# Branch gates by one Strassen level with token sums kept in DRAM, the Fourier transform beside them and its projection behind them; retention in step and a joined qkv projection

## The chip, the cores and the metric

The kernel runs on one core of a Trainium2 chip. The metric is device time in microseconds (us) of one execution, the median of the runs shown. All data are float32. A product of two float32 matrices is made of three TensorE matmuls over a high and a low part (hi·hi, hi·lo, lo·hi), each part in the chip's fp32r form; `split` makes the parts, the high one by a copy on ScalarE (ACT), the low one by a subtraction on VectorE (DVE).

## The reference

One layer of a hybrid backbone on 1024 tokens of width 1024 (and 256 context tokens). Cut to what matters here:

```python
h = modulate(rms_norm(x, norm1_w), sh1, sc1)
q, k, v, g, f = split_proj(h @ w_in)            # 8 heads of 64 (q, k) and 128 (v); f is 512 wide
o = bidir_retention(rope(q), rope(k), v, ...)   # chunks of 128, starts from the context's states
ret_d  = (layer_norm_per_head(o) * silu(g)) @ w_ret_out
four_d = real(fft2(f, tokens and groups of 128)) @ w_four_out
gates  = sigmoid(h @ w_branch_gate + b)         # (1024, 2048): g_r, g_f
x = x + g1 * ((g_r * ret_d + g_f * four_d) @ w_out)
x = x + g2 * conv_ffn(modulate(rms_norm(x, norm2_w), sh2, sc2))
return rms_norm(x, final_norm_w)
```

sh1, sc1, g1, sh2, sc2, g2 are six vectors of 1024 that come from `silu(c) @ w_mod + b_mod`.

## The kernel before, in words

Everything is kept transposed (channels on the 128 partitions, tokens along the free axis), in two halves t of 512 tokens. The normalized input is `hT[t]`, a hi and a lo tile of 8 channel blocks by 512 tokens each, in the pool `ap` (four buffers with the tag A, all taken by hT).

The program's stages, in the order in which they are written:

1. Norm, modulation and the first head pair's q, k and v (to about 85 us of the trace).
2. `gate_proj(0)`, the context's keys and values (`ctx_proj`, `ctx_state`, four pairs), the decay tables (`decay_tables`, `expo`).
3. For the head pairs p = 1 to 3: q and k (`in_proj` with `w_qk`), then v (`in_proj` with `w_v`), each as matmuls of 128 tokens by 256 columns; `gate_proj(p)`; `retention(p)`. The scheduler lays retention of pair p beside the projections of pair p + 1.
4. The retention gates `gr` (L588, L592): 8 blocks of 128 channels, each 2 halves x 8 channel blocks x 3 parts = 48 matmuls of 512 tokens; the sigmoid goes to `sr_d` in DRAM.
5. The Fourier branch: projection `f`, `spectra`, `transform`, `nyquist`; its result z stays in SBUF. Then, in turns, a Fourier gate `gf` (48 matmuls of 512) and a block `fo` of the projection of z (24 matmuls), multiplied on DVE and written to `t_d` in DRAM.
6. "re", the retention projection, merged with `sr_d` and `t_d`; then "wo", the output projection with the residual, and the second norm, for each half.
7. The FFN: the up projection by one level of Strassen's scheme in Winograd's form (`up_mm`, `chain` at L775: seven chains of 12 matmuls of 512 for a pair of blocks), the convolution, the gate; then the down projection by the same scheme (L1054).

The vectors g1, sc2, sh2 and g2 are made on DVE: `mod_dot` makes one of their 32 blocks from 512 KB of `w_mod` (a DMA into the raw buffer `wraw`, two multiply-and-sum passes of 512, one small step). `run_mods(n)` takes the next n of them; the table MODS says how many are taken where. When the block of g1 or g2 is complete, TensorE transposes the 8 columns (`gt`) and the row goes to DRAM.

The order on each engine is made by a scheduler at build time from the written program; each engine then runs its own list in order, and so do the two queues that issue DMAs (SP, and POOL where the code says `G.dma_start`). Weights come through three raw buffers `wraw` of 512 KB (`wload`, L102) into two buffers `whi` and two `wlo`.

Of the kernel before, what the change touches and what calls it, by code (L numbers as in the profile page):

```python
# [16 lines left out]
P = 128  # L17
# [14 lines left out]
MODS = (2, 2, 2, 2)  # L32
# [11 lines left out]
def tile_block(ctx: ExitStack, tc: tile.TileContext, a: dict, out: bass.AP):  # L44
# [49 lines left out]
    sr_d = dr.tile([KD, P, L], F32, name="sr_d")  # L94
    t_d = dr.tile([KD, P, L], F32, name="t_d")
# [259 lines left out]
    T2 = {"t2": 3, "t2b": 3}  # L355
    with tc.tile_pool(name="rp", bufs=1) as rp:
# [29 lines left out]

        def in_proj(wk, t, ps):
            for n in range(4):
                for k in range(KD):
                    mm3(ps[:, n, :], pick(hT[t], ALL, k, blk(n)), wk(k), k == 0, k == KD - 1)  # L390
# [39 lines left out]
        def retention(p, qkr, vt, tab, sg):  # L430
# [37 lines left out]
            for t in range(2):  # L468
                scs = [rt(f"sc{p}{i}{t}") for i in range(2)]
                for n in range(4):  # L470
                    c = blk(4 * t + n)
                    for i in range(2):
                        T.matmul(scs[i][:, blk(n)], kT[blk(i, QK), c], qT[blk(i, QK), c], start=True, stop=True)
                for i in range(2):
                    h, sc = 2 * p + i, scs[i]
                    pt = t2(rp, f"pt{h}{t}").rearrange("p (n c) -> p n c", n=4)
                    tt(pt, sc.rearrange("p (n c) -> p n c", n=4),
                       tab[:, i, :].unsqueeze(1).broadcast_to([P, 4, P]), MUL)
                    o = rt(f"o{h}{t}")
                    for n in range(4):  # L480
                        T.matmul(o[:, blk(n)], pt[:, n, :], vt[t][:, n, blk(i)], start=True, stop=False)
                        T.matmul(o[:, blk(n)], qfb[i][:, blk(4 * t + n)], ss[i][:, 4 * t + n, :],
                                 start=False, stop=True)
                    st = rp.tile([P, 4, 6], F32, tag="st", bufs=2, name=f"st{h}{t}")
# [3 lines left out]
                    for n in range(4):  # L488
                        V.bn_stats(st[:, n, :], o[:, blk(n)])
                        V.bn_aggr(mv[:, n, :], st[:, n, :])  # L490
# [3 lines left out]
                    on = t2(rp, f"on{h}{t}").rearrange("p (n c) -> p n c", n=4)  # L494
                    for n in range(4):
                        S.activation(on[:, n, :], o[:, blk(n)], AF.Identity, bias=nm[:, n:n + 1],  # L496
                                     scale=rs[:, n:n + 1])
                    ot = rt(f"ot{h}{t}")
                    for n in range(4):
                        T.transpose(out=ot[:, blk(n)], in_=on[:, n, :], identity=ident)  # L500
                    ro = t2(rp, f"rr{h}{t}")
                    tt(ro, ot, sg[i][:, blk(t, 512)], MUL)
                    dma(r_d[h][:, blk(t, 512)], ro)
# [54 lines left out]

        retention(0, qkr, vt, tab, sg)
        for p in range(1, 4):  # L560
            qkr, vt = qkv_tiles(p)
            w = wload_k(a["w_qk"], p - 1, "wqk")
            for t in range(2):
                ps = mmt(f"qk{p}{t}").rearrange("p (n c) -> p n c", n=4)
                in_proj(lambda k: pick(w, ALL, k), t, ps)
                S.copy(qkr[t], ps)
                rope(qkr[t], qkr[t], 4 * t, 4, f"{p}{t}")
            w = wload_k(a["w_v"], p, "wv")
            for t in range(2):
                ps = mmt(f"v{p}{t}").rearrange("p (n c) -> p n c", n=4)  # L570
                in_proj(lambda k: pick(w, ALL, k), t, ps)
                S.copy(vt[t], ps)
            tab = decay_tables(p)
            run_mods(MODS[0])
            sg = gate_proj(p, wload_k(a["w_g"], p, "wg"))
            run_mods(MODS[1])
            retention(p, qkr, vt, tab, sg)
        for t, n in ((bbg, "bbg"), (convw, "convw"), (convb, "convb")):
            dma(t, a[n])

        def gate(w, js, cs, ss, name):
            pss = [mmt(f"{name}{c}") for c in cs]
            for t in range(2):
                for j, ps in zip(js, pss):
                    for k in range(KD):
                        mm3(ps[:, blk(t, 512)], pick(w, ALL, k, blk(j)), pick(hT[t], ALL, k), k == 0, k == KD - 1)
            for c, ps, s in zip(cs, pss, ss):
                S.activation(s, ps, AF.Sigmoid, bias=bbg[:, c:c + 1])  # L588

        for i in range(4):  # L590
            w = wload_k(a["w_bg"], i, "wbr")
            for j in range(2):  # L592
                s = t4(f"sr{2 * i + j}", (L,))
                gate(w, (j,), (2 * i + j,), (s,), "gr")
                dma(sr_d[2 * i + j], s)
                run_mods(MODS[2])

    with tc.tile_pool(name="zp", bufs=1) as zp, tc.tile_pool(name="fp", bufs=1) as fp:
        z = tuple(zp.tile([P, 4, L], F32R, name=f"z{n}") for n in "hl")
        fourc = zp.tile([P, 1664], F32, name="fourc")  # L600
        cdft = zp.tile([P, 256], F32, name="cdft")[:, 0:129]
        x64 = fp.tile([P, 128], F32, name="x64")[:, 0:20].rearrange("p (a b) -> p a b", b=4)
        dma(fourc, a["fourc"])
        dma(cdft, a["cdft"])

        def spectra(g, ps, X):
            f = fp.tile([P, L], F32, tag="f", name=f"f{g}")
            S.copy(f, ps)
            eo = fp.tile([P, L], F32, tag="eo", name=f"eo{g}")
            F = fp.tile([P, L], F32, tag="F", name=f"F{g}")  # L610
# [42 lines left out]
        def transform(pr_, X):  # L653
# [10 lines left out]
            q = fp.tile([P, 512], F32, tag="q", bufs=1, name=f"q{pr_}")  # L664
            S.copy(q, pn)
            zf = fp.tile([P, L + 128], F32, tag="zf", bufs=1, name=f"zf{pr_}")
# [5 lines left out]
            S.copy(zf[:, L:L + 1], pc[:, 384:385])  # L672
            for i, src in enumerate((zf[:, 0:L], zf[:, L:0:-1])):
                split(z[0][:, 2 * pr_ + i, :], z[1][:, 2 * pr_ + i, :], src)

        def nyquist():
# [7 lines left out]
            zn = tuple(fp.tile([P, L], F32R, tag=t, name=f"zn{t}")[0:4] for t in ("eo", "F"))  # L684
# [6 lines left out]
        def place(zn):  # L691
            for i in range(2):
                for g in range(4):
                    r = 64 * (g % 2)
                    dma(z[i][r:r + 1, 2 * (g // 2) + 1, :].bitcast(F32), zn[i][g:g + 1, :].bitcast(F32))

        for i in range(2):
            w = wload_k(a["w_f"], i, "wf")
            X = fp.tile([P, 9, P], F32, tag="X", name=f"X{i}")
            for j in range(2):  # L700
                ps = mmt(f"f{i}{j}")
                for t in range(2):
# [582 lines left out]
```

## Time and profile before

| | us |
|---|---|
| median of 3 runs | 1548.14 (1547.11 to 1548.68) |
| the profiled execution, whole | 1546.61 |
| its span, first to last instruction | 1544.8 |
| TensorE (PE) busy in the span | 1506.2 (97%) |
| VectorE (DVE) busy | 1034.1 (67%) |
| ScalarE (ACT) busy | 632.9 (41%) |
| granted TensorE clock, mean | 0.995 of full |

The span is what the trace covers; the profiled execution's own time is 1.8 us more. PE's busy time covers its pipelined matmuls and so does not tell how dense they follow each other; for that one reads when they start. DVE and ACT work one instruction at a time, so that their busy time is also their load.

### The profile page before, as it was taken

The page shows a single profiled execution, that of the slowest core. Times are in us where ns is not written, and L with a number is a line of the kernel's source. Part 1 is how long each engine was busy: PE and PEld are TensorE (multiplying, and loading weights), DVE is VectorE, ACT ScalarE, POOL GpSimd, SP SyncE. Part 2 cuts the span into 40 slices and gives each one's busy share as a digit, 9 for nine tenths or more (in the row PEclk, how much of TensorE's full clock was granted, in tenths as well). Part 3 has the DMA queues.
Part 4 walks back from the last instruction along what each step waited for, and adds up shares of the span by engine and source line. Part 5 has one row for each costly group of instructions (what it writes and reads, how often), then busy time and mean ns, then how long its engine had stood idle before and what let it go on. Part 6 is the DMA issues. An engine that isn't in the chain of part 4 may idle for free.

```text
span 1544.8 us, 20455 instructions
## 1 busy us (share of the span) xinstructions
PE 1506.2 (97%) x7806; PEld 1268.8 (82%) x7806; DVE 1034.1 (67%) x1926; ACT 632.9 (41%) x1084; POOL 71.8 (5%) x115
## 2 busy tenths in 40 slices
PE   7999999999999999999999979999999999999996
PEld 3789989999888888888888867888888888878885
DVE  5586847558463373115458698888787888697676
ACT  6565123132222232112255465545454555454453
POOL 0000000000000000000000000100000000000001
PEclk9999999999999999999999999999999999999999
DMA  9235221222443331218377342322323223595332
GB/s 367 93 131 168 86 69 62 83 83 90 141 140 136 120 109 56 82 69 304 105 255 261 137 164 82 136 88 98 121 89 116 101 103 130 178 400 186 127 90 109
DMA packets 77779, 211.13 MB, mean 137 GB/s; under 512 B 9760, under 2 KB 14128, under 8 KB 77680
## 3 DMA queue, kind: packets, MB, share of 16 engines
q1 hardware_dynamic: 71520, 189.63, 36.0%
q0 software_dynamic: 6160, 20.19, 3.3%
q8 instruction: 61, 1.00, 0.3%
q14 instruction: 38, 0.31, 0.1%
HBM read 166.49 MB, written 43.26 MB: 136 GB/s over the span
## 4 chain that ended last, share of the span: by engine, by line
PE 77%; DVE 10%; DMA 9%; issue 2%; ACT 1%; SPq 0%; POOL 0%; DVEq 0%; ACTq 0%
PE x L775 15%; PE y L775 7%; PE dx L1054 6%; PE z L775 3%; DMA mt<-wmT 3%; DVE ss L59 2%; PE dz L1054 2%; PE dy L1054 2%; PE re L117 2%; PE gf L117 2%; PE g L119 2%; PE re L118 2%; PE re L119 2%; PE gf L118 2%; PE gf L119 2%
## 5 line engine op out<-in xcount | busy, mean ns | idle before, releaser
L775 PE MATMUL x<-s,wt 128*128 128x512 f32 x528 | 128.3, 389 | 0.0
L775 PEld LDWEIGHTS x<-s,wt 128*128 128x128 f32 x528 | 99.1, 188 | 20.5
L1054 PE MATMUL dx<-ob,oa 128*128 128x512 f32 x432 | 99.5, 390 | 1.2 <-DVE ob L50 1.2
L1054 PEld LDWEIGHTS dx<-ob,oa 128*128 128x128 f32 x432 | 80.9, 188 | 18.9 <-DVE ob L50 2.2
L50 DVE TENSOR_TENSOR wt<-t,wt 128x512 fp32r<-128x512 f32 x84 | 57.4, 687 | 46.0 <-ACT wt L99 46.0
L181 DVE SCALAR_TENSOR_TENSOR mt<-mt,silrow 128x512 f32<-128x512 f32 x64 | 41.7, 689 | 66.1 <-DMA mt<-wmT 66.1
L99 ACT CAST oa<-pr 128x512 fp32r<-128x512 f32 x69 | 43.0, 624 | 88.2 <-PE dx L1054 30.6
L50 DVE TENSOR_TENSOR oa<-pr,oa 128x512 fp32r<-128x512 f32 x69 | 47.4, 688 | 31.5 <-ACT oa L99 31.4
L775 PE MATMUL y<-s,wt 128*128 128x512 f32 x264 | 65.3, 390 | 2.7 <-DVE s L50 1.9
L99 ACT CAST wt<-t 128x512 fp32r<-128x512 f32 x84 | 52.2, 623 | 35.9 <-PE x L775 29.3
L775 PE MATMUL x<-a,wt 128*128 128x512 f32 x264 | 63.5, 389 | 1.0 <-DVE cv L50 1.0
L775 PE MATMUL z<-a,wb 128*128 128x512 f32 x252 | 64.4, 389 | 0.0
L775 PE MATMUL y<-s,wb 128*128 128x512 f32 x264 | 63.4, 389 | 0.0
L775 PE MATMUL x<-a,wb 128*128 128x512 f32 x252 | 62.1, 392 | 0.0
L496 ACT ACTIVATE on<-o,nm,rst 128x128 f32<-128x128 f32 x64 | 24.0, 455 | 92.8 <-DVE nm L59 92.8
L59 DVE SCALAR_TENSOR_TENSOR t<-ca,convw,t 128x1023 f32<-128x1023 f32 x44 | 56.3, 1279 | 7.7 <-ACT t L982 7.6
L775 PEld LDWEIGHTS y<-s,wt 128*128 128x128 f32 x264 | 49.5, 188 | 13.6 <-DVE s L50 2.2
L1054 PE MATMUL dy<-ob,oa 128*128 128x512 f32 x264 | 60.5, 389 | 0.0
L775 PEld LDWEIGHTS x<-a,wt 128*128 128x128 f32 x264 | 49.5, 188 | 11.7 <-DVE cv L50 1.5
L775 PEld LDWEIGHTS y<-s,wb 128*128 128x128 f32 x264 | 49.6, 188 | 10.3
L1054 PEld LDWEIGHTS dy<-ob,oa 128*128 128x128 f32 x264 | 49.6, 188 | 10.3
L59 DVE SCALAR_TENSOR_TENSOR t<-cv,convw,t 128x1023 f32<-128x1023 f32 x44 | 56.2, 1278 | 0.0
(954 smaller groups left out, 4125.4 us busy)
## 6 DMA issues: line engine op xcount, KB each, us to landing
pr<-p_d SPq DMA_DIRECT2D x69, 256.0 KB, 2.9
mt<-wmT SPq DMA_DIRECT2D x32, 512.0 KB, 3.8
d<-w_down SPq DMA_DIRECT2D x44, 256.0 KB, 5.5
p_d<-t POOLq DMA_DIRECT2D x43, 256.0 KB, 2.9
p_d<-s POOLq DMA_DIRECT2D x34, 256.0 KB, 3.2
xh<-xT SPq DMA_DIRECT2D x8, 512.0 KB, 7.3
r_d<-rr SPq DMA_DIRECT2D x16, 256.0 KB, 3.7
sr_d<-sr SPq DMA_DIRECT2D x8, 512.0 KB, 4.2
```

The source lines that it names most:

```text
L50: V.tensor_tensor(out=out, in0=in0, in1=in1, op=op)
L59: V.scalar_tensor_tensor(out=out, in0=in0, scalar=s, in1=in1, op0=op0, op1=op1)
L99: S.copy(hi, src)
L117: T.matmul(o, l[0], r[0], start=first, stop=False)
L118: T.matmul(o, l[0], r[1], start=False, stop=False)
L119: T.matmul(o, l[1], r[0], start=False, stop=last)
L181: V.scalar_tensor_tensor(out=raw[:, c], in0=raw[:, c], scalar=1.0, in1=silrow[:, c], op0=MUL, op1=MUL, accum_out=acc[:, h:h + 1])
L496: S.activation(on[:, n, :], o[:, blk(n)], AF.Identity, bias=nm[:, n:n + 1], scale=rs[:, n:n + 1])
L775: T.matmul(ps, x[:, l, k], y[:, r, k], start=(first and k == 0 and l + r == 0), stop=(k == 3 and l == 1), skip_group_check=True)
L1054: T.matmul(ps[n], x[l][:, blk(n)], y[r], start=(first and l + r == 0), stop=(l == 1), skip_group_check=True)
```

## The change

The change does five things to the middle of the program (stages 2 to 6).

- **Gates by Strassen.** Two of the 16 gate blocks (0 and 4) are made as before. The other 14 are made in 7 pairs (m, m + 4), by the scheme that the FFN uses: 7 chains of 12 matmuls for a pair instead of 96. For this it needs four combinations of hT (s1 to s4, over halves of tokens and of channels) and of the weights.
- **Sums in DRAM.** `sums_k` makes s1 to s4 on DVE, 10 subtractions or additions of 128x512 for each of 4 channel blocks, and POOL writes them to `s_d`. `s_load` brings them back before the gates; s4 takes the place of a quarter of hT.
- **The Fourier transform beside the gates, its projection behind.** The four blocks of f go to DRAM, and spectra, transform and nyquist are laid between the gate pairs; z goes to `z_d` in DRAM, and is read back into the buffers of `hT[0]` after the last pair has used it. The finished gates go to DRAM (`sr_d`, `sf_d`), and the eight blocks `fo` follow in a row, each with its `sf_d` read back.
- **Retention in step, joined qkv.** The two heads of a pair go through each step of retention one after the other instead of head by head. For p = 1 to 3, q, k and v come from one weight of 512 columns.
- **`mod_dot` elsewhere.** None beside the qkv projections; 3 after each of the retentions 1 to 3, 3 after the first gates, 1 after each of two f blocks, 10 beside the gates, and the last 8 within "re". The stores of sr, sf, z and t move from the SP queue to POOL. The scratch space for POOL's DMA descriptors falls to 4096 bytes per partition.

```diff
-MODS = (2, 2, 2, 2)
+MODS = {"ctx": 0, "ret": 3, "gr": 3, "f": 1, "g": (1, 1, 1, 1, 1, 2, 3), "re": 1}
+SUMS = ((), (0, 1), (2, 3), ())
...
+        def sums_k(k):
+            A11, A12, A21, A22 = ([v[:, k + 4 * h].bitcast(F32) for v in hT[t]] for t in range(2) for h in range(2))
...
+            comb("s1", A21[0], (ADD, A22[0]), (ADD, A21[1]), (ADD, A22[1]))
+            comb("s2", s["s1"], (SUB, A11[0]), (SUB, A11[1]))
+            comb("s3", A11[0], (SUB, A21[0]), (ADD, A11[1]), (SUB, A21[1]))
+            comb("s4", A12[0], (SUB, s["s2"]), (ADD, A12[1]))
...
-            w = wload_k(a["w_qk"], p - 1, "wqk")
+            ws = [wload_k(a["w_qkv"], 2 * (p - 1) + q, f"wqkv{p}", 4) for q in range(2)]
...
+                            mm3(pss[n // 2][:, n % 2, :], pick(hT[t], ALL, 4 * q + k, blk(n)), pick(ws[q], ALL, k),
+                                q + k == 0, q + k == 4)
...
+        def g_mm(i):
+            (x, z), y = gbank[i], rt(f"gy{i}")
+            ca, cv = rows(f"gca{i}"), rows(f"gcv{i}")
+            lo, hi = slice(0, 512), slice(512, 1024)
+            S.copy(ca[:, lo], x)
+            tt(ca[:, lo], ca[:, lo], z, ADD)
+            chain(x, gops[i, "t2"], hops["s2"], False)
+            S.copy(cv[:, lo], x)
+            chain(y, gops[i, "t1"], hops["s1"], True)
+            S.copy(cv[:, hi], y)
+            chain(x, gops[i, "t3"], hops["s3"], False)
+            tt(cv[:, hi], cv[:, hi], x, ADD)
+            chain(y, gops[i, "b22"], hops["s4"], False)
+            tt(cv[:, lo], cv[:, lo], y, ADD)
+            chain(x, gops[i, "t4"], hops["a22"], False)
+            S.copy(ca[:, hi], x)
+            return ca, cv
...
+        steps = [lambda: spectra(0), lambda: spectra(1), lambda: (transform(0), spectra(2)),
+                 lambda: spectra(3), lambda: (transform(1), place(nyquist())), lambda: None, lambda: None]
+        g_first(1)
+        g_prep(1)
+        s_load("s4")
+        for i in range(1, 8):
+            cs = g_mm(i)
+            if i < 7:
+                g_first(i + 1)
+                g_prep(i + 1)
+            g_out(i, cs)
+            steps[i - 1]()
+            run_mods(MODS["g"][i - 1])
+
+        z = [ap.tile([P, 4, L], F32R, tag="A", name=f"z{n}") for n in "hl"]
+        for k in range(4):
+            for i in range(2):
+                dma(z[i][:, k].bitcast(F32), z_d[i][k])
+        for m in range(KD):
+            if m % 4 == 0:
+                wfo = wload_k(a["w_four"], m // 4, "wfo", 4)
+            sf = rows(f"sf{m}")
+            dma(sf, sf_d[m])
...
+            tt(sf, sf, ps, MUL)
+            G.dma_start(t_d[m], sf)
...
+                    if t == 0:
+                        run_mods(MODS["re"])
```

`g_first(i)` loads half of a pair's weights and runs the first two chains; `g_prep(i)` makes the combinations of the weights on DVE; `g_out(i)` applies the sigmoid and stores.

Where the scheduler puts the sums: on DVE, behind the norm of the context and ahead of the first rope (`ro`), the list was

```order
L50 TENSOR_TENSOR silrow<-silrow,uc 128x256
L56 TENSOR_SCALAR small<-small 128x32
L50 TENSOR_TENSOR ro_844<-qkr_832,ropec 128x512
L50 TENSOR_TENSOR ro_845<-qkr_832,ropec 128x512
L50 TENSOR_TENSOR ro_848<-qkr_832,ropec 128x512
L50 TENSOR_TENSOR ctt_815<-ctt_815,silrow 128x256 x4
```

and it now begins (names that begin with s_ are the sums, _0 the channel block):

```order
L51 TENSOR_TENSOR silrow<-silrow,uc 128x256
L51 TENSOR_TENSOR s_0_2455<-h1h 128x512
L51 TENSOR_TENSOR s_0_2455<-s_0_2455,h1l 128x512 x2
L57 TENSOR_SCALAR small<-small 128x32
L51 TENSOR_TENSOR s_0_2456<-s_0_2455,h0h 128x512
L51 TENSOR_TENSOR s_0_2457<-h0h,h1h 128x512
L51 TENSOR_TENSOR s_0_2456<-s_0_2456,h0l 128x512
L51 TENSOR_TENSOR s_0_2457<-s_0_2457,h0l 128x512
L51 TENSOR_TENSOR ro_872<-qkr_860,ropec 128x512
```

Although they are written behind retentions 1 and 2, all 40 sums stand in stage 2, the last of them ahead of the last context weight's low part.

On PE, at the end of the context projections, the list was

```order
L119 MATMUL vc_1360<-wvc2hi,hc1l 128x256
L117 MATMUL vc_1432<-wvc3hi,hc0h 128x256
L118 MATMUL vc_1432<-wvc3lo,hc0h 128x256
L119 MATMUL vc_1432<-wvc3hi,hc0l 128x256
L117 MATMUL vc_1432<-wvc3hi,hc0h 128x256
```

and is now (s is the product that makes the context's state, kcfb its keys as DVE scales them):

```order
L124 MATMUL vc_1390<-wvc2hi,hc1l 128x256
L122 MATMUL qkv_1819<-wqkv10hi,h0h 128x512
L122 MATMUL qkv_1820<-wqkv10hi,h0h 128x512
L437 MATMUL s_1301<-vc_1245,kcfb_1296 128x128 x4
L122 MATMUL vc_1462<-wvc3hi,hc0h 128x256
L123 MATMUL vc_1462<-wvc3lo,hc0h 128x256
```

The first state product (of pair 0) stood in the second pair's projection; it now stands ahead of the fourth's, with two matmuls of qkv before it, and waits for `kcfb`, which DVE makes behind the sums.

On the SP queue, around the end of the gates, the list was

```order
L106 DMA wbf7r_5964<-w_bg 128x1024
L728 DMA t_d<-s_5435 128x1024
L728 DMA t_d<-s_5436 128x1024
L728 DMA t_d<-s_5630 128x1024
L106 DMA wbf7r_5968<-w_bg 128x1024
L728 DMA t_d<-s_5631 128x1024
L751 DMA rraw_6235<-r_d 128x2x512
```

and behind four loads of z (blocks 0 and 2, hi and lo), the first of which waits for PE to finish with `hT[0]`, it now is

```order
L181 DMA mt_5473<-wmT 128x1024
L181 DMA mt_5479<-wmT 128x1024
L111 DMA wfo0r_5497<-w_four 128x1024
L111 DMA wfo0r_5501<-w_four 128x1024
L111 DMA wfo1r_5623<-w_four 128x1024
L852 DMA zh<-z_d_116 128x1024
L852 DMA zh<-z_d_118 128x1024
L857 DMA sf_5505<-sf_d_95 128x1024
L111 DMA wfo1r_5627<-w_four 128x1024
L852 DMA zl<-z_d_120 128x1024
L890 DMA rraw_5853<-r_d 128x2x512
L852 DMA zl<-z_d_122 128x1024
```

So all of z, both halves of the weights of `fo`, two blocks of `mod_dot` and the first raw block of r are issued after the last pair's first two chains.

## Rows read from the trace of the kernel before

**Rows 1.** The page, part 1: busy time, share of the span, instructions.

```profile
PE 1506.2 (97%) x7806; PEld 1268.8 (82%) x7806; DVE 1034.1 (67%) x1926; ACT 632.9 (41%) x1084; POOL 71.8 (5%) x115
```

**Rows 2.** Windows: stretch, its us, busy us (x instructions), PE clock, DMA share, GB/s.

```profile
core 0: us, PE busy (x) PEld busy (x) DVE busy (x) ACT busy (x) POOL busy (x), PEclk, DMA share, GB/s
0.00:40.00 40.00, 28.83 (x193) 16.24 (x194) 21.36 (x62) 26.96 (x62) 0.70 (x6) 1.00 0.97 369
...
75.00:145.00 70.00, 69.62 (x458) 63.78 (x457) 51.36 (x122) 38.05 (x69) 0.00 (x0) 1.00 0.46 149
145.00:420.00 275.00, 272.45 (x1968) 254.01 (x1967) 180.01 (x469) 74.35 (x134) 12.57 (x12) 1.00 0.28 89
420.00:520.00 100.00, 99.73 (x512) 83.08 (x512) 43.90 (x124) 27.15 (x44) 4.74 (x5) 1.00 0.35 119
520.00:760.00 240.00, 240.00 (x1104) 199.10 (x1103) 95.82 (x181) 57.14 (x91) 0.00 (x0) 1.00 0.37 128
760.00:880.00 120.00, 119.76 (x552) 99.33 (x551) 79.47 (x120) 61.24 (x100) 3.26 (x6) 1.00 0.65 219
880.00:940.00 60.00, 49.81 (x218) 40.33 (x217) 53.13 (x98) 34.54 (x66) 2.69 (x2) 0.94 0.35 119
940.00:1320.00 380.00, 380.00 (x1678) 314.77 (x1677) 321.33 (x418) 194.21 (x285) 37.88 (x70) 1.00 0.31 109
...
1520.00:1545.00 25.00, 12.21 (x54) 9.77 (x53) 13.32 (x28) 3.92 (x10) 2.59 (x4) 0.84 0.22 84
```

**Rows 3.** The chain that ended last: start us, us, what (x instructions).

```profile
887.68 2.73 PE x L775 x12
...
1472.38 29.92 PE dz L1054 x132
```

**Rows 4.** Timeline of PE in the v projection, a matmul each: start, us.

```profile
282.83 0.28 PE L117 MATMUL v<-wv2hi,h1h 128*128 128x256 f32 x1
...
285.11 0.28 PE L118 MATMUL v<-wv2lo,h1h 128*128 128x256 f32 x1
```

**Rows 5.** Timeline of DVE at the start of stage 2; brackets: idle before, and why.

```profile
78.29 0.18 DVE L56 TENSOR_SCALAR small<-small 128x32 f32<-128x32 f32 x1 [3.24 <-DMA small<-expc]
78.99 1.90 DVE L50 TENSOR_TENSOR ro<-qkr,ropec 128x512 f32<-128x512 f32 x3 [0.52 <-ACT qkr L523]
```

**Rows 6.** The tile kcfb: one kind of instruction each, first and last start.

```profile
L50 DVE TENSOR_TENSOR kcfb<-kcs,small x16: 284/285/293, 123.8 to 142.8; 128x128 f32<-128x128 f32 x16
```

**Rows 7.** Groups by line, all of the trace: busy us, mean ns, idle before and releasers.

```profile
L775 PE MATMUL y<-s,wt 128*128 128x512 f32 x264 | 65.3, 390 | 2.7 <-DVE s L50 1.9 <-ACT s L99 0.8
```

**Rows 8.** Windows, columns as in the second group: three shorter stretches.

```profile
700.00:740.00 40.00, 40.00 (x178) 33.14 (x177) 19.04 (x23) 8.75 (x11) 0.00 (x0) 1.00 0.79 289
1360.00:1380.00 20.00, 20.00 (x90) 16.56 (x89) 19.62 (x33) 10.33 (x19) 0.00 (x0) 1.00 1.05 406
900.00:940.00 40.00, 36.27 (x160) 29.39 (x159) 33.92 (x60) 22.99 (x43) 0.00 (x0) 0.97 0.26 86
```

**Rows 9.** The tile mt of mod_dot: first and last start, waits, landings.

```profile
L181 DVE SCALAR_TENSOR_TENSOR mt<-mt,silrow x64: 678/689/695, 148.0 to 552.2; 128x512 f32<-128x512 f32 x64
...
  DMA mt<-wmT: 66.1, 27
...
DMA to landing us min/median/max: 3.4/3.8/5.8
```

**Rows 10.** DMA issues: queue, x transfers, KB each, median us to landing.

```profile
p_d<-s POOLq DMA_DIRECT2D x34, 256.0 KB, 3.2
...
r_d<-rr SPq DMA_DIRECT2D x16, 256.0 KB, 3.7
...
sr<-sr_d SPq DMA_DIRECT2D x8, 512.0 KB, 8.1
tf<-t_d SPq DMA_DIRECT2D x8, 512.0 KB, 8.8
```

More of the change, by code (lines that the diff above doesn't have):

```diff
@@ L353, in tile_block, with f_proj @@
         wg0 = wload_k(a["w_g"], 0, "wg")
-    T2 = {"t2": 3, "t2b": 3}
+    T2 = {"t2": 6, "t2b": 3}
+    wf = []
+    def f_proj(g):
+        if g % 2 == 0:
+            wf[:] = [wload_k(a["w_f"], g // 2, "wf")]
+        ps = mmt(f"f{g}")
+        for t in range(2):
+            for k in range(KD):
+                mm3(ps[:, blk(t, 512)], pick(wf[0], ALL, k, blk(g % 2)), pick(hT[t], ALL, k), k == 0, k == KD - 1)
+        return ps
     with tc.tile_pool(name="rp", bufs=1) as rp:
@@ L590, in tile_block @@
[L590 to L602, printed above, removed]
+                for k in range(KD):
+                    mm3(ps[:, blk(t, 512)], pick(w, ALL, j, k), pick(hT[t], ALL, k), k == 0, k == KD - 1)
@@ new lines, in tile_block, with chain @@
+            sr = t4(f"sr{m}", (L,))
+            S.activation(sr, ps, AF.Sigmoid, bias=bbg[:, m:m + 1])
+            G.dma_start(sr_d[m], sr)
+        run_mods(MODS["gr"])
+        for g in range(2):
+            f = t4(f"fc{g}", (L,))
+            S.copy(f, f_proj(g))
+            G.dma_start(f_d[g], f)
+            run_mods(MODS["f"])
+    def chain(ps, x, y, first):
+        for k in range(4):
+            for l, r in ((0, 0), (0, 1), (1, 0)):
+                T.matmul(ps, x[:, l, k], y[r][:, k], start=(first and k == 0 and l + r == 0),
+                         stop=(k == 3 and l == 1), skip_group_check=True)
@@ L603, in tile_block, with s_load @@
         dma(fourc, a["fourc"])
         dma(cdft, a["cdft"])
[L606 to L610, printed above, removed]
+        def s_load(n):
+            for q in range(2):
+                raw = wide(f"{n}r{q}").rearrange("p (k n) -> p k n", k=2)
+                dma(raw, s_d[n][q].rearrange("p (k n) -> p k n", k=2))
+                split(hops[n][0][:, 2 * q:2 * q + 2], hops[n][1][:, 2 * q:2 * q + 2], raw)
@@ new lines, in tile_block, with wpair, both, g_load @@
+        for g in (2, 3):
+            f = rows(f"fc{g}")
+            S.copy(f, f_proj(g))
+            G.dma_start(f_d[g], f)
+        for n in ("s2", "s1", "s3"):
+            s_load(n)
+        gops, graw, gbank = {}, {}, {}
+        def wpair(i, n, tag):
+            return wp.tile([P, 2, 2, 512], F32R, tag=tag, name=f"gw{n}{i}")
+        def both(t, src):
+            split(t[:, :, 0], t[:, :, 1], src)
+            return [t[:, j].rearrange("p l (k n) -> p l k n", k=4) for j in range(2)]
+        def g_load(i, s):
+            graw[i, s] = wp.tile([P, 1024], F32, tag="wraw", bufs=3, name=f"gw{i}r{s}").rearrange("p (h n) -> p h n", h=2)
+            dma(graw[i, s], a["w_bg"][i, s].rearrange("p (h n) -> p h n", h=2))
@@ new lines, in g_out, with spectra @@
+        def g_out(i, cs):
+            for j in range(2):
+                m = i % 4 + 4 * j
+                c = 8 * (i // 4) + m
+                S.activation(cs[j], cs[j], AF.Sigmoid, bias=bbg[:, c:c + 1])
+                G.dma_start(sf_d[m] if i // 4 else sr_d[m], cs[j])
+        def spectra(g):
+            if g % 2 == 0:
+                Xs.append(gp.tile([P, 9, P], F32, tag="X", name=f"X{g // 2}"))
+            X = Xs[-1]
+            f, eo, F = wide(f"f{g}"), wide(f"eo{g}"), wide(f"F{g}")
+            dma(f, f_d[g])
@@ L770, in tile_block @@
     bank = {}
-    def chain(ps, x, y, first):
-        for k in range(4):
-            for l, r in ((0, 0), (0, 1), (1, 0)):
-                T.matmul(ps, x[:, l, k], y[:, r, k], start=(first and k == 0 and l + r == 0),
-                         stop=(k == 3 and l == 1), skip_group_check=True)
     def wop(i, name, src, t=None):
```

208 lines of the change are left out of this document (120 added, 88 removed).

## The prediction

> **What bounds the kernel now.** I read the page's busy times first: PE is busy 97% of the span, DVE 67%, ACT 41%, POOL 5% [rows 1]. Since an average hides stages, I cut the span into windows next [rows 2]. PE fills every stretch from 75 to 880 us and the FFN's 940 to 1320 us to 99% or more; only the start, the second norm at 880 to 940 and the end have holes. So between 75 and 880 us, where the change works, time is the number of matmuls times their spacing, and no wait is left there to remove. Nothing is bought by moving work on the other engines, unless it makes a new wait.
>
> The spacing is read where matmuls stand in a gapless row, from start to start, since their own durations (280 ns and more) overlap. With 512 columns: 29.92 / 132 = 0.2267 us, and 2.73 / 12 = 0.2275 [rows 3]. With 256 columns: 19 intervals from 282.83 to 285.11, 0.120 us each [rows 4]. A matmul of half the columns thus costs 53% of a whole one, not half.
>
> The other engines in these stretches: DVE has 18.6 us idle of 70 in stage 2 (75 to 145 us), 95 of 275 beside the qkv projections, 144 of 240 beside the Fourier branch [rows 2]. The DMA engines moved 89 to 219 GB/s there.
>
> **What goes.** A pair of gate blocks took 2 x 48 = 96 matmuls of 512 columns and takes 7 x 12 = 84. Seven pairs save 7 x 12 = 84 matmuls: 84 x 0.2267 = **-19.0 us**. The two plain blocks, f, the transform, `fo` and everything from "wo" on keep their counts.
>
> q, k and v of the pairs 1 to 3 were 1152 matmuls of 256 columns and become 576 of 512: 1152 x 0.120 = 138.2 against 576 x 0.2267 = 130.6, **-7.7 us**. Together -26.7.
>
> The Trainium skill, page "TensorE: Matmul & The Clock Gate", section "Back-to-back issue gap", gives for a lone stream about N/2.4 + 2.5 ns. That is 216 and 109 ns, and an estimate by this page would make the join worth 1152 x 0.109 - 576 x 0.216 = 1.2 us. The rows (227 and 120 ns) are dearer by 11 ns in both shapes, and they carry my sum.
>
> **What is added, and what hides it.**
>
> *Sums.* 40 DVE operations of 128x512, 0.605 us each: the three `ro` take 1.90 us, of which the last is about 0.69 [rows 5]. That is 24.2 us. They are written behind retentions but stand in stage 2, where DVE has 18.6 us idle [rows 2], part of it waits that stay, such as 3.24 for `expc` [rows 5]. DVE must therefore get late by at least 24.2 - 18.6 = 5.6 us and at most 24.2. What is late next is `kcfb`: first at 123.8, then every (142.8 - 123.8)/15 = 1.27 us [rows 6]. PE now wants the first two ahead of the fourth context V projection, which is 48 matmuls of 256 before the end of the stage: 145 - 48 x 0.120 = 139.2, and 0.5 for two matmuls of qkv, 139.7. With half of the idle time used, DVE is late by 24.2 - 9.3 = 14.9, the second `kcfb` ends at 123.8 + 14.9 + 2.5 = 141.2, and PE waits 1.5 us. The bounds are 0 (all idle time used: 131.9) and 10.8 (none used: 150.5). The weights' low parts, which stand between the sums, can each cost PE a little as well, so I take **+2.5**, range 0 to 11. Everything in PE's list stands behind that product.
>
> *Combinations of the gates' operands.* Weights and sums are split and combined on DVE and ACT beside 7 x 84 x 0.2267 = 133 us of chains. The FFN does the same by the same scheme with DVE 85% busy and PE full [rows 2]; there 22 groups of chains waited 2.7 us in all [rows 7], 0.12 a group, or about 1 for the seven pairs. Entering that loop cost 40 - 36.27 = 3.7 us [rows 8], behind a norm, which the gates don't have. I take **+1**, range 0 to 4. If DVE were late, the next chain's PSUM bank would be.
>
> *Stores on POOL.* POOL is busy 5% [rows 1], and a store issued there lands as fast as one of SP: 3.2 us against 3.7 for 256 KB [rows 10]. The 16 stores of sums stand ahead of the first retention's steps on POOL and wait for the sums, so `rst` there is late if the sums are; what the trace doesn't show is the price of the smaller descriptor space. Bounds 0 and 3 (one landing, [rows 10]); I take 0, as POOL's stores of p_d cost PE nothing visible beside the projections.
>
> *Retention in step* reorders matmuls in a stretch where PE already idles only 2.55 of 275 us [rows 2]: it can give at most that and lose a few; I take 0.
>
> *Entrance to `fo`.* This is the dangerous place. The first load of z waits until PE has done the last pair's first two chains (call it T0), because it overwrites `hT[0]`. Queued behind it on SP are two `mt`, four raw weight blocks, the other z blocks, `sf` and the first r. PE has 84 matmuls of the last chains and the first `fo` products to do, and by my count of its list needs the last block of zl after 84 + 20 = 104 matmuls: 104 x 0.2267 = 23.6 us. Until then 16 loads of 0.524 MB and some 1.3 MB of stores, 9.7 MB, must pass. At the 406 GB/s that this trace reached [rows 8] that is 23.9 us, and a landing adds about 2, so 2.3 us late. At the 289 GB/s of 700 to 740 us [rows 8] it is 33.6, and 12 late. The 406 stood beside a DMA share of 1.05, a queue that was full as it is here, so I take **+2**, range 0 to 12. Behind the late z stand all eight `fo` on PE, and behind them "re".
>
> The Trainium skill, page "DMA: Bandwidth & Descriptors", section "Specifications", puts the limit of one core on HBM at about 358 GB/s; by an estimate from it the 9.7 MB take 27.1 us and the entrance costs 5.5. The trace's 406 GB/s over 20 us lies above that figure, so that I don't use it.
>
> *mod_dot in "re".* All 32 were done by 552 us, and DVE waited 66.1 us in 27 of its 64 steps for `mt` [rows 9], 2.4 each, with nobody waiting for DVE. Now eight stand in "re", which lasts about 192 x 0.2267 = 43.5 us, and PE's `gt` for g1 comes just before "wo". One `mt` needs 3.8 to land [rows 9] and two passes of some 0.7, so that eight through one buffer take 8 x (3.8 + 1.4) = 42 us: barely hidden. I take **+0.5**, range 0 to 14 (the landings at 5.5 us; [rows 10] has 8.1 and 8.8 for 512 KB of sr and tf in this stretch).
>
> **The sum.** -26.7 + 2.5 + 1 + 2 + 0.5 = -20.7. The profiled execution took 1546.6 (span 1544.8 and 1.8 around it); so 1525.9 for a like one, and the median lies 1.5 above the profiled one: 1527.4, rounded to **1527**.
>
> **The rivals.** A measurement of this kernel tells 0.2%, 3.1 us, from no change.
>
> 1. *All is hidden.* The gates' chains run as dense as the FFN's, and z and sums come in time: 1548.1 - 26.7 = 1521.4, 1519 to 1523.5 with the idle time that retention in step could give back. For it: 144 us idle on DVE beside the Fourier branch. Against it: the two places where my own count has the supplier later than PE.
>
> 2. *The mods or the retention are late.* If `mt` lands in 5.5 us as neighbours do, the eight need 8 x 6.9 = 55 us against 43.5, and "wo" starts up to 12 to 14 late: 1527 + 13 = 1540. The same size follows if the sums delay the first retention by all their 24.2 us less what slack PE's list has. For it: 66.1 us of waits for `mt` [rows 9]. Against: two or three of the eight can start during `fo`, since three raw buffers exist.
>
> 3. *DMA becomes the bound from the load of z to "wo", and this ends slower.* From T0 on, about 106 us of PE work stand to "wo" (84 matmuls of chains, 192 of `fo`, 192 of "re": 468 x 0.2267 = 106), and 55 loads and 12 stores of 0.524 MB, 35 MB, belong to them: 330 GB/s. Before, that work was spread: z stayed in SBUF and the mods were done. At 289 GB/s [rows 8] the stretch lasts 121 us, 15 more, and with the stalls at stage 2 the time is 1538 to 1541. The point from which the kernel is slower than before is 35 / (106 + 26.7) = 264 GB/s; at the 219 GB/s of the 760 to 880 stretch [rows 2] it is 160 us, 54 more, 1575. Against it: 289 and 406 are what was asked for, not a ceiling, except the 406 at a share of 1.05.
>
> 4. *Two half-wide matmuls cost one whole.* If the 0.120 us is a wait for weights or banks that comes back in the joined form (a weight of 512 columns fills two raw blocks), the join gives 0: -19.0 + 6 = -13, and 1535. This is also where the page on TensorE would lead, within 1.2 us. Against it: 1968 instructions in 272.45 us [rows 2], with 1152 x 0.120 and 144 x 0.2267 taken off, leave 0.15 for each of the rest, so the 0.120 fits.
>
> **How the numbers follow.** The forecast (3 to 12 us of new stalls, 1524 to 1534) has 0.60: the counts are certain, the spacings are read from long rows, and only the stalls are open. Rival 1 has 0.13, rival 2 0.10, rival 3 0.12 (of which 0.05 is slower than before, 0.02 lands within 0.2%), rival 4 0.05. The range 1519 to 1541 holds the forecast, rivals 1 and 4 nearly whole, and half of 2 and 3, over 0.8; its low end is the sum without stalls and 2.5 of retention, its high end the entrance to `fo` or the mods at their upper bound. Faster by over 0.2%: 0.60 + 0.13 + 0.05 + 0.09 of rival 2 + 0.04 of rival 3 = 0.91; same 0.04; slower 0.05.
>
> **What would show it.** In the profile after, PE has 84 + 576 = 660 instructions fewer than 7806. Dense chains of gates start every 0.2267 us, joined qkv matmuls too. A gap of PE ahead of the fourth context V projection with DVE `kcfb` as releaser is the sums' price; a gap near the last pair or first `fo`, released by a DMA of zh or zl, is the entrance's; `gt` released late by DVE `mt` is the mods'. The prediction is wrong if PE idles more than some 12 us in new places between 75 and 880 us, if the DMA share stands at 0.9 or more through `fo` and "re" while PE waits, or if PE's clock, 0.94 in the stretch with PE's idle time of 880 to 940 [rows 2], falls in another place after such a gap and makes it dearer.

## The result and the profile after

The changed kernel takes **1530.37 us** (median of 4 runs, 1528.08 to 1533.15) beside 1548.41 for the kernel before on the same chips: ratio 0.9883, 95% interval 0.9866 to 0.9900, 18 us less. The forecast was 1527, range 1519 to 1541. The profiled execution took 1528.08 us, with a span of 1526.3, against 1546.61 and 1544.8. One execution, the profiled one of the run mods_fo below, took 2141.8 us at a mean granted clock of 0.655 and is left out of every comparison.

Part 1 of the page after, to be held against [rows 1]:

```profile
PE 1481.6 (97%) x7146; PEld 1220.5 (80%) x7146; DVE 1109.5 (73%) x2039; ACT 668.0 (44%) x1146; POOL 102.9 (7%) x175
```

PE has 7806 - 7146 = 660 instructions fewer, as counted. Its share is 97% as before and so tells nothing of what was lost. The windows of the changed kernel do, cut at its own stages: stage 2; the projections with the plain gates and f; the seven gate pairs; the projection of z; "re", "wo" (columns as in [rows 2]).

```profile
75.00:145.00 70.00, 66.96 (x421) 59.95 (x419) 65.44 (x144) 37.21 (x66) 8.85 (x16) 1.00 0.63 197
145.00:484.00 339.00, 339.00 (x1840) 286.79 (x1840) 219.78 (x551) 102.88 (x193) 19.05 (x21) 1.00 0.30 96
484.00:638.00 154.00, 149.04 (x688) 122.03 (x687) 102.29 (x225) 64.45 (x109) 15.14 (x29) 0.99 0.53 176
638.00:690.00 52.00, 47.53 (x206) 38.05 (x205) 25.77 (x37) 11.96 (x13) 4.80 (x9) 1.00 0.96 353
690.00:870.00 180.00, 180.00 (x819) 149.17 (x818) 120.69 (x189) 79.97 (x127) 3.83 (x7) 1.00 0.68 230
```

A window less PE's busy time in it is PE's idle time: 3.04, 0, 4.96, 4.47 and 0 us, together **12.5**. The stretches from 75 to 880 us of [rows 2] have 0.38 + 2.55 + 0.27 + 0 + 0.24 = 3.4. So the matmuls should bring -26.7 by count, the idle time brought +9.0, and -17.7 of the profiled difference of -18.5 is accounted for. The FFN's first chain, which stood at 887.68 us [rows 3], confirms it: it comes 17.65 us earlier.

```profile
870.03 2.73 PE x L640 x12
```

The waits of PE from 80 to 880 us after the change say where (engine, line, what released it: total, times, longest):

```profile
PE fo L122 <- DMA zh<-z_d: 2.7, 1, 2.7
PE gx L640 <- ACT gcv L719: 1.6, 1, 1.6
PE g L124 <- DVE wg0lo L51: 1.4, 1, 1.4
PE xa L764 <- DVE F L51: 1.3, 1, 1.3
PE qkv L122 <- ACT wqkv10hi L104: 1.1, 1, 1.1
PE gx L640 <- DVE gca L51: 1.0, 1, 1.0
PE fo L123 <- DMA zl<-z_d: 1.0, 1, 1.0
...
PE s L437 <- DVE kcfb L51: 0.2, 1, 0.2
```

Three places: stage 2 (`wg0lo`, `wqkv10hi`, `kcfb`), the gates (gca, gcv and the transform's F), and the entrance to `fo` (zh, zl). What DVE and ACT do ahead of these waits stands in the chain that ended last, cut from 551 to 651 us (start, us, what):

```profile
551.74 1.24 DVE gwc L51
553.00 4.82 DMA mt<-wmT
557.83 1.31 DVE mt L186 x4
...
560.27 1.22 DVE zl L51
...
564.09 6.35 DMA f<-f_d
...
597.89 2.73 PE gx L640 x12
...
616.80 6.15 DMA mt<-wmT
...
624.91 5.96 DMA mt<-wmT
...
632.24 6.24 DMA wfo0r<-w_four
...
639.58 1.24 DVE wfo0lo L51
640.83 0.38 SPq L890
...
641.30 9.52 DMA zl<-z_d
```

DVE stands in its list before an `mt` that has not landed, with the gates' combinations queued behind it. `mt` also holds the raw buffer that the next weight needs (`wfo0r` follows `mt`), and at the end z itself is late. L890 is the first load of r. It wants a raw buffer too and goes out when `wfo0lo` has freed one; the last block of z stands right behind it in SP's list, goes out at 641.30 us and needs 9.52 us to land. The DMA engines there (three windows of the changed kernel):

```profile
615.00:630.00 15.00, 14.67 (x65) 11.80 (x64) 11.91 (x27) 7.18 (x15) 3.56 (x8) 1.00 0.97 354
630.00:645.00 15.00, 12.18 (x53) 9.44 (x51) 6.62 (x14) 5.14 (x7) 3.59 (x7) 1.00 1.01 380
645.00:660.00 15.00, 13.35 (x56) 10.41 (x57) 9.12 (x8) 7.66 (x8) 1.41 (x3) 1.00 1.02 384
```

They are full for 45 us, at 354 to 384 GB/s. So z is held up twice, by its place in the queue and by full DMA engines.

### The profile page after: what moved, and what is told of

It is laid out like the page before. It is cut to its first block, busy times and chain, and to the rows that moved or that the text cites. A ratio compares the mean times of both kernels' runs of the same rounds, so it can differ in the third digit from the quotient of the medians.

```text
span 1526.3 us, 19489 instructions
## 1 busy us (share of the span) xinstructions
PE 1481.6 (97%) x7146; PEld 1220.5 (80%) x7146; DVE 1109.5 (73%) x2039; ACT 668.0 (44%) x1146; POOL 102.9 (7%) x175
## 4 chain that ended last, share of the span: by engine, by line
PE 85%; DMA 8%; DVE 4%; ACT 1%; issue 1%; SPq 0%; DVEq 0%; POOL 0%; ACTq 0%
PE x L640 15%; PE y L640 8%; PE dx L1189 6%; PE z L640 3%; PE gx L640 3%; PE qkv L123 3%; PE qkv L124 3%; PE qkv L122 3%; PE dz L1189 2%; PE dy L1189 2%; PE g L124 2%; PE re L122 2%; PE re L123 2%; PE wo L122 2%; PE wo L123 2%; PE wo L124 2%
## 5 line engine op out<-in xcount | busy, mean ns | idle before, releaser
L640 PEld LDWEIGHTS x<-a,wb 128*128 128x128 f32 x252 | 48.0, 191 | 10.0
```

Source lines behind the costliest of these rows:

```text
L640: T.matmul(ps, x[:, l, k], y[r][:, k], start=(first and k == 0 and l + r == 0), stop=(k == 3 and l == 1), skip_group_check=True)
```

## The experiments

Differences to the changed kernel are taken between the two ratios to the kernel before, times 1548 us, since the runs were on several chips; with intervals of some +-0.0015 each, such a difference is good to about 3.4 us. "Gaps" in the expectations were counted from start to start of neighbouring matmuls, beyond the spacing of [rows 3, 4].

**Two halves for a joined matmul.** In the qkv loop:

```diff
-mm3(pss[n // 2][:, n % 2, :], pick(hT[t], ALL, 4 * q + k, blk(n)), pick(ws[q], ALL, k), ...)
+for c in range(2):
+    l, r = pick(hT[t], ALL, 4 * q + k, blk(n)), pick(ws[q], ALL, k, blk(c, 256))
+    o = pss[n // 2][:, n % 2, blk(c, 256)]
+    (three matmuls of 256 columns)
```

> Each joined matmul of 512 columns of q, k and v is issued as two of 256 on the same loaded operands; nothing else is changed. Theory (price of columns, 0.120 against 0.2267 us): 1152 x 0.120 - 576 x 0.2267 = 7.7 us more than the changed kernel, about 1538. Rival (two half-wide matmuls cost what one whole does): within 1.5 us of the changed kernel, about 1531.

Measured 1540.56 us, ratio 0.9951 (0.9938 to 0.9965): 10.5 us more. The rows of PE in its projections (a matmul each) keep the price of before:

```profile
251.82 0.28 PE L610 MATMUL qkv<-wqkv22hi,h0h 128*128 128x256 f32 x1
...
253.86 0.28 PE L610 MATMUL qkv<-wqkv22hi,h0l 128*128 128x256 f32 x1
```

17 intervals in 2.04 us are 0.120 each. The theory holds; the rival that two halves cost one whole doesn't. Nor does the estimate of 1.2 us from the Trainium skill, page "TensorE: Matmul & The Clock Gate", section "Back-to-back issue gap"; the section itself calls that formula the gap of an isolated matmul, and these stand in a stream.

**Plain gates.** Pairs 1 to 7 as eight chains on the same operands:

```diff
-SUMS = ((), (0, 1), (2, 3), ())
+SUMS = ((), (), (), ())
...
+chain(x, b11, hops["a11"], True);  chain(x, b21, hops["a12"], False)
+chain(z, b11, hops["a21"], True);  chain(z, b21, hops["a22"], False)
+chain(y, b12, hops["a11"], True);  chain(y, b22, hops["a12"], False)
+chain(x, b12, hops["a21"], True);  chain(x, b22, hops["a22"], False)
```

> The seven gate pairs are made as eight plain chains of 12 on the same weights in the same place; no sums, no combinations, s4 not loaded, everything else as changed. Theory: 84 matmuls more, 19.0 us, less the 2.8 us that the sums cost PE in stage 2 and 0 to 4 of the gaps among the gates (DVE has 60 operations less there): 12 to 16 us more than the changed kernel, 1542 to 1547. Rival (the scheme's sums, combinations and loads give back most of what it saves): under 8 us more, below 1539.

Measured 1538.84 us, ratio 0.9940 (0.9928 to 0.9953): 8.8 us more (its profiled execution, 1540.27, is 12.2 above the changed kernel's). Its windows in stage 2 and among the gates:

```profile
75.00:145.00 70.00, 69.42 (x447) 63.20 (x446) 52.79 (x126) 37.95 (x69) 0.00 (x0) 1.00 0.46 138
...
482.00:649.00 167.00, 166.78 (x780) 138.48 (x779) 53.47 (x137) 54.27 (x86) 15.57 (x30) 1.00 0.47 155
```

PE idles 0.58 and 0.22 us there instead of 3.04 and 4.96; at `fo` it idles 4.23, about as in the changed kernel. So of the 19.0 us that the scheme saves in matmuls, 7.2 went into waits that come with its sums and combinations. The median lies between the theory's 12 and the rival's 8; the interval decides for neither.

**Retention head by head.** The loop of retention as before the change, the rest changed.

```diff
-for i in range(2):  (scores of both heads)
-for i in range(2):  (products of both heads) ...
+for i in range(2):  (scores, product, statistics, transpose, store of one head)
```

> Retention goes head by head again, as before the change; all else stays changed. Theory (the three waits of PE for scores and transposes beside the old projections, 1.2 + 1.0 + 0.8 us, went because the two heads alternate): they come back, 2 to 4 us more than the changed kernel. Rival (they went because the joined projection offers other matmuls in between): within 1 us of the changed kernel.

Measured 1567.19 us, ratio 1.0124 (1.0109 to 1.0139): 37 us more than the changed kernel, and slower than the kernel before. Neither theory nor rival had this. The transposes `ot` at retention's end, first and last start (before the change, after it, and head by head), and the first chain of the gates head by head:

```profile
L500 PE MATMUL ot<-ident,on x64: 270/272/329, 186.8 to 518.4; 128*128 128x128 f32 x64
```
```profile
L518 PE MATMUL ot<-ident,on x64: 270/271/331, 194.2 to 460.8; 128*128 128x128 f32 x64
```
```profile
L511 PE MATMUL ot<-ident,on x64: 270/272/475, 195.0 to 510.7; 128*128 128x128 f32 x64
...
L632 PE MATMUL gx<-h0h,gwa x112: 387/389/796, 513.0 to 656.9; 128*128 128x512 f32 x112
```

Head by head, the last transposes come at 510.7 us and the gates start at 513.0 (484 in the changed kernel); in step they come at 460.8. In the kernel before the same slow pace ended at 518.4, beside the 100 us of plain gates `gr` (420 to 520 us, PE busy 99.73 [rows 2]), which covered it. The change leaves two of these eight blocks, and by its code the seven pairs' buffers lie in a pool that opens where retention's closes. PE's largest wait from 380 to 540 us head by head, and its windows of the last retention and of the gates:

```profile
PE ot L511 <- ACT on L507: 8.0, 4, 3.4
```
```profile
380.00:513.00 133.00, 114.76 (x594) 93.98 (x592) 60.51 (x172) 31.82 (x63) 11.50 (x12) 0.96 0.20 67
513.00:675.00 162.00, 151.12 (x688) 123.56 (x689) 110.11 (x233) 71.73 (x117) 15.67 (x30) 0.97 0.62 207
```

PE idles 18.24 and 10.88 us there. From 75 us to the FFN's first chain, which now comes at 907.22, it idles 37.5 us where the changed kernel idles 12.5. That is 25 of the 37 us; in the other 12 PE is busy, but slower, at a granted clock of 0.96 and 0.97 in these two windows. That `gr` was the cover is argued from these times: no run has the joined projections and head by head retention with all eight plain blocks behind them, so that the longer projections of the kernel before may have been part of the cover.

**The kernel before with retention in step alone**, the counterpart (with six buffers t2 and the small descriptor space that make room).

> The kernel before with retention in step alone (with the six buffers t2 and the smaller descriptor space that make room for them); gates, qkv and everything else as before. Theory (in the kernel before retention has the long gates behind it to end in, so its pace costs only the three waits of PE of 1.2 + 1.0 + 0.8 us beside the projections): 2 to 4 us less than before, 1544 to 1546. Rival A (the waits are only moved): within 1.5 us of before. Rival B (its pace already bounded the kernel before): over 8 us less, below 1540.

Measured 1547.33 us beside 1546.53: ratio 1.0008 (0.9999 to 1.0017). Rival A holds. Retention in step is worth nothing in the kernel before, where long gates stand beside its end, and 37 us in the changed one.

**Where the ten blocks of `mod_dot` stand.** Beside retention:

```diff
-MODS = {"ctx": 0, "ret": 3, "gr": 3, "f": 1, "g": (1, 1, 1, 1, 1, 2, 3), "re": 1}
+MODS = {"ctx": 0, "ret": 5, "gr": 5, "f": 2, "g": (0, 0, 0, 0, 0, 0, 0), "re": 1}
```

> The ten blocks of mod_dot that run beside the gate pairs are moved to the retentions (5 instead of 3 each), the first gates (5 instead of 3) and the f blocks (2 instead of 1 each); the eight in re stay. Theory (DVE's waits for mt, and the raw buffers that mt holds, make the gaps of PE among the gate pairs and most of the one ahead of fo): the 5.7 us of gaps among the gates go and 2 to 4 of the 4.9 at fo, 6 to 9 us less than the changed kernel, 1521 to 1524, minus what the moved blocks cost beside retention (0 to 4). Rival (the gap at fo is the bytes of z in too short a time, and the gates wait for the Fourier transform): the entrance keeps over 4 us and the total gains under 3.

Measured 1529.69 us, ratio 0.9881 (0.9868 to 0.9895): the same. Its windows from stage 2 to the end of `fo`:

```profile
75.00:145.00 70.00, 65.81 (x403) 58.80 (x402) 63.91 (x144) 36.49 (x65) 8.81 (x16) 0.99 0.62 196
145.00:407.00 262.00, 260.98 (x1428) 221.10 (x1427) 185.83 (x482) 72.41 (x144) 12.12 (x12) 1.00 0.31 95
407.00:494.00 87.00, 83.63 (x433) 70.14 (x432) 50.95 (x123) 30.41 (x51) 6.93 (x9) 0.98 0.43 147
494.00:635.00 141.00, 141.00 (x667) 117.15 (x665) 87.80 (x173) 63.51 (x107) 15.05 (x29) 1.00 0.45 154
635.00:690.00 55.00, 53.14 (x226) 43.20 (x225) 25.26 (x34) 12.81 (x14) 4.78 (x9) 0.97 0.87 332
```

The gain and its price are both seen. The gates run without a gap and `fo` idles 1.86 instead of 4.47, none of it for z: PE waits 1.6 for a gate's `gcv` and 0.2 for `wfo0lo`. So `mt` was needed for both gaps, with all of z's bytes still to load, and the rival fails at `fo`. It isn't the only thing needed: the gates' gap also goes without the scheme's sums and combinations (plain_gates, 0.22) and, below, with `mt` in place (late_zwhole, 0.25). The total is the rival's (under 3 us): 1.0 and 3.4 us of idle time come up beside the projections and the last retention, where PE now waits 3.4 for retention's states, and stage 2 idles 4.19 instead of 3.04. Moved to the projection of z instead:

```diff
+            run_mods(MODS["fo"])     # 1 behind each fo block, "gr": 5, "g": none
```

> The ten blocks of mod_dot beside the gate pairs go elsewhere: eight to the projection of z (one behind each fo block), two behind the first gates. Theory (in the gates DVE waits for mt, and the weights' raw buffers behind mt): the gaps among the gates (6.1 us over the stretch from the first f block's end to fo) go as they did with the blocks beside retention, the gap at fo falls to about 2, and the 4.2 MB more of loads during fo cost at most 2: 4 to 9 us less than the changed kernel, 1521 to 1526. Rival (ten blocks cost some 7 us wherever they stand, since each takes one of the three raw buffers that PE's weights need): 1529 to 1533.

Measured 1535.99 to 1537.73 us in four executions, ratio 0.9927 (0.9914 to 0.9941): 7 us more, worse than theory and rival. No trace of these four was kept, so that none shows why; that eight more loads of 0.52 MB meet DMA engines which the windows above show full is an argument, not a finding.

**The sums later.** Their buffers from retention's pool t2, so that they can't stand ahead of it:

```diff
-s = {n: rp.tile([P, 512], F32, tag="sq", bufs=3, name=f"{n}_{k}") for n in s_d}
+s = {n: t2(rp, f"{n}_{k}") for n in s_d}
```

> The 40 sums take their buffers from the pool that retention works with, so that they stand on DVE where they are written, behind the retentions 1 and 2, and not in stage 2. Theory (they delay DVE's tables in stage 2 and nothing else): the gaps of 2.9 us in stage 2 fall under 1, 1.5 to 3 us less than the changed kernel, 1527 to 1529. Rival (retention is paced by DVE, and its tail delays the gates): 24 us of DVE work beside it make PE wait at the last retention, 2 to 8 us more, 1532 to 1538.

Measured 1524.10 us, ratio 0.9843 (0.9830 to 0.9857): 6.2 us less than the changed kernel. That is more than the theory's 1.5 to 3, and the rival of a late retention falls. Its windows of stage 2, the projections, the gates and `fo`:

```profile
75.00:145.00 70.00, 69.60 (x455) 63.64 (x454) 51.52 (x123) 37.79 (x68) 0.00 (x0) 1.00 0.46 146
145.00:398.00 253.00, 253.00 (x1368) 213.85 (x1367) 177.83 (x450) 70.93 (x139) 17.79 (x21) 1.00 0.29 89
...
482.00:638.00 156.00, 150.53 (x686) 122.70 (x685) 106.16 (x229) 69.18 (x114) 15.05 (x29) 0.98 0.57 193
638.00:685.00 47.00, 46.33 (x204) 37.80 (x204) 24.05 (x32) 10.99 (x12) 4.78 (x9) 1.00 0.93 358
```

Stage 2 idles 0.40 instead of 3.04, and the sums, now from 297 to 421 us, are hidden beside the last projections and retention (PE idles 0 and 0.71 us in the windows up to 482). The gap at `fo` shrinks too (0.67), while the gates keep theirs (5.47). At `fo` PE no longer waits for z: the last block of z goes out at 636.6 us instead of 641.3. What lets it go out earlier no run separates.

**z at `fo`: queue or bytes.** On ACT's queue, past SP's:

```diff
-dma(z[i][:, k].bitcast(F32), z_d[i][k])
+S.dma_start(z[i][:, k].bitcast(F32), z_d[i][k])
```

> The eight loads of z are issued on ACT's queue, not on SP's behind the loads of mt, of the weights of fo and of sf. Theory (z is late because of what is queued ahead of it): the gap of 4.9 us at fo falls under 2.5, about 3 us less than the changed kernel, 1526 to 1529. Rival (z is late because its bytes and the others' share the DMA engines in too short a time): the gap stays over 4, within 1.5 us of the changed kernel; if ACT is held by the wait for PE, it grows.

Measured 1528.96 us, ratio 0.9869 (0.9854 to 0.9884), not told apart from the changed kernel. The end of its chain, and PE's window behind the gap:

```profile
631.99 5.53 DMA wfo0r<-w_four
637.62 7.53 DMA zh<-z_d
...
645.99 4.96 PE gx L640 x12
```
```profile
645.00:650.00 5.00, 4.80 (x11) 3.80 (x12) 0.00 (x0) 0.08 (x1) 0.54 (x1) 0.50 1.02 374
```

PE waits 3.4 us for zh there, so the rival's sign (a gap that stays) is seen. But the edit didn't free z. ACT's list also goes in order: the load that PE waits for goes out at 637.62, right behind ACT's own wait for `wfo0r`, and the last block of z at 644.0. One held list took the place of the other, so the run doesn't acquit the queue.

As one part, split behind the load:

```diff
-zs = [wide(f"z{n}{pr_}{i}", F32R) for n in "hl"]  (split, then two stores)
+zs = wide(f"z{pr_}{i}") if i else zf               (one store)
...
+zr = wide(f"zr{k}")
+dma(zr, z_d[0][k])
+split(z[0][:, k], z[1][:, k], zr)
```

> z goes to DRAM and back as one part, 2.1 MB each way and not 4.2, and is split into its high and low part after the load (ACT and DVE, 4 blocks of 1.05 + 1.2 us); else the changed kernel. Theory (the gap at fo is bytes: the DMA engines are full, at a share of 0.97 to 1.02, from 615 to 675 us): 2.1 MB less at some 380 GB/s is 5.5 us earlier, the gap falls from 4.9 us to under 2, 3 us less than the changed kernel, 1526 to 1528. Rival (what counts is when PE frees the buffers, and the landing behind it): the gap stays over 4 or grows by the split's 2.3 us, 1530 to 1533.

Measured 1521.36 us, ratio 0.9836 (0.9822 to 0.9849): 7.3 us less. Its windows of the gates and `fo`, and the loads of z (first and last issue):

```profile
485.00:632.00 147.00, 144.42 (x680) 119.61 (x679) 99.61 (x215) 66.37 (x112) 11.02 (x21) 1.00 0.52 173
632.00:681.00 49.00, 48.94 (x216) 40.23 (x215) 25.29 (x34) 12.41 (x13) 4.79 (x9) 1.00 0.85 310
```
```profile
L851 SPq DMA_DIRECT2D zr<-z_d x4: 320/354/424, 602.5 to 616.1; - x4
```

Of the gap at `fo` 0.06 us stay, as the theory said. But the edit halves the bytes and does more: the loads go into a spare buffer `zr` instead of `hT[0]`, so that they start at 602.5 us, 12 before PE has done the last pair's first two chains (614.4), and the last goes out at 616.1 instead of 641.3. It also takes z's splits out of the gates' stretch, where PE's idle time fell from 4.96 to 2.58. So this doesn't show that the bytes made the gap; bytes, wait for `hT[0]` and place in the queue went together.

**Cures together.** `mt` in a buffer of its own, with the sums late:

```diff
-raw = wp.tile([P, 1024], F32, tag="wraw", bufs=3, name=f"mt{i}")
+raw = const.tile([P, 1024], F32, tag="mtraw", bufs=1, name=f"mt{i}")
```

> The sums as in sums_late, and mt in a buffer of its own and no longer in one of the three raw buffers that the weights use. Theory (among the gates PE waits because the weights' loads wait for a raw buffer that mt holds): the gaps among the gates fall from 6.1 us to under 3, 3 us or more below sums_late. Rival (what holds PE up is DVE's wait for mt itself, in order ahead of the weights' combinations): the gaps stay over 5, or grow, as one buffer loads one mt at a time; within 2 us of sums_late or above.

Measured 1523.11 us, ratio 0.9838 (0.9824 to 0.9851), the same as sums_late. Among its gates PE idles 0.4 us, but 4.3 beside the projections, where the free buffer lets the blocks come earlier: all 32 start by 269 us. So this doesn't tell the buffer from the place. The 3 us that the theory asked for beyond sums_late didn't come. With z as one part on top:

> Three cures together: sums late, mt in a buffer of its own, z as one part. Theory (each takes away gaps of its own place): mt_own's gap of 2.2 us at fo goes, 1520 to 1522. Rival (at fo PE then waits for the split of z or for the weights instead): within 1.5 us of mt_own, 1522 to 1525.

1519.52 us, ratio 0.9823 (0.9809 to 0.9836): not clear of mt_own by the times, but `fo` idles 0.11 us instead of 1.90, as the theory said. And without the buffer:

> Two cures together: the sums behind the retentions, z as one part; mt in the weights' raw buffers as changed. Theory (the gaps of stage 2 and those of the gates and fo are separate losses that add): 6 us of sums_late and 9 of z_whole, 1514 to 1518. Rival (both shorten the same wait, that of the gates' end for DVE and the DMA engines, so that only the longer one counts): 1519 to 1523.

1520.25 us, ratio 0.9819 (0.9801 to 0.9836): the median lies in the rival's range, and the theory that the two gains add missed. Both runs beat the changed kernel by 9 to 10 us, but not z_whole alone by more than the noise. In the window of the gates the two cures do together what neither does alone (0.25 us beside 5.47 and 2.58). At `fo` a wait of 2.6 us comes back, now for a gate's `gca` on ACT and not for z:

```profile
481.00:629.00 148.00, 147.75 (x695) 122.40 (x694) 105.24 (x222) 71.54 (x117) 11.03 (x21) 1.00 0.57 189
```
```profile
PE fo L122 <- ACT gca L727: 2.6, 1, 2.6
```

## Why the prediction was right, point by point

- **Gates, -19.0.** Right as a count, and the chains run at the spacing of [rows 3] (12 in 2.73 us in the chain above). With what the scheme brings in waits it nets 9 to 12.
- **Join, -7.7.** Right: 10.5 +-3.4 when undone, at 0.120 us each.
- **Sums, +2.5.** Right in size, and DVE is late as worked out; the path to PE was another, so that the size is in part luck. `kcfb` was to start 14.9 us later than 123.8; after the change its row reads

```profile
L51 DVE TENSOR_TENSOR kcfb<-kcs,small x16: 281/284/289, 139.6 to 151.3; 128x128 f32<-128x128 f32 x16
```

  so 15.8 later, and stage 2 idles 3.04 - 0.38 = 2.7 us more. PE's wait, though, is for `wqkv10hi` and `wg0lo` (2.5 together) rather than for `kcfb` (0.2 of the 1.5 forecast). The prediction had named the low parts only as something more that it gave no figure.
- **Combinations, +1.** Mis-sized: 4.96. The step "the FFN does the same by the same scheme" left out what the FFN doesn't have beside it: `mod_dot` in DVE's order and in the weights' raw buffers, z's splits, and loads of f. Without `mt` (mods_early), without sums and combinations (plain_gates), or with later sums and fewer splits (late_zwhole) the gap is gone; which of the chain's links costs what stays open.
- **Entrance to `fo`, +2.** Mis-sized: 4.47. The place was right, and full DMA engines were there, but at some 377 GB/s instead of 406. From the end of the last pair's first two chains (620.9 us) to the landing of z (650.8) 11.3 MB passed and not 9.7, and the landing, taken at 2 us, was 9.52 for the last block. And the prediction costed the queue as bytes alone: it left out that the last load of z stands behind a load of r that waits for a raw buffer until 640.8. 0.7 of the 4.47 is a wait for a gate's `gca`. The Trainium skill, page "DMA: Bandwidth & Descriptors", section "Specifications", with its 358 GB/s would have given 5.5, nearer than the 2.3 worked out from the row. The rate measured here lies above its figure, and the gap isn't of the rate alone, so that this doesn't speak for it.
- **`mod_dot` in "re", +0.5.** None: PE is busy 180.00 of 180 from 690 to 870 us. Rival 2 fell.
- **Retention in step, 0.** True of the edit alone (1.0008), wrong as a reading of the change: the step named no cover. By the times above `gr` was the cover of retention's pace, the change removes most of it, and head by head the kernel is slower than before. The total came out right because the change carries its own remedy; the prediction hadn't seen that it was needed. None of the rivals had this.
- **The sum.** New stalls of 6 were forecast and 9.0 came. That is a difference: 12.1 came in the three places, at the edge of the 12 from which the prediction called itself wrong, and 3.1 of idle time of the kernel before went, beside its projections, its last retention and "wo", where the sum had taken 0. So the total is nearer than its two mis-sized terms by luck. The clock, the third sign, fell in a new place too, behind the gaps among the gates: it read 0.74 from 570 to 575 us. Rival 3's stretch moved 353 GB/s through `fo` and 230 beyond, and only the entrance suffered.

## What to carry to other kernels

A dense engine's gain is certain as a count, but each supplier made to work in less time can give some back: here 7 of 19 us. When a long stage is shortened or removed, ask first what was ending under it. And before costing an edit at nothing, undo it in thought in the new kernel, not in the old: the same loop order was worth 0 in one and 37 us in the other. A run that moves a load to another queue tests the queue only if the load then goes out earlier: look at the issue time before reading the result.

## What the runs showed of the hardware

With loads and stores mixed, DMA engines at a share of 0.97 to 1.02 moved 354 to 384 GB/s, against 406 in [rows 8] at 1.05. The landings of `mt` took 3.4 to 10.2 us in the changed kernel, median 4.6, against 3.4 to 5.8, median 3.8 [rows 9]. A gap can cost more than its length: in z_act PE idled 3.4 us for zh, and in the 5 us from 645 on the granted clock read 0.50, the level of 1.2 GHz; the chain of 12 there took 4.96 us instead of 2.73. In the changed kernel, behind 2.7 us at the same place, the clock read 1.00.
